# A hybrid decoder block on one core: another order of the projection tiles, and two side jobs as lanes issued by POOL

## The chip, the cores and the metric

The kernel runs on one core of one Trainium2 chip. The metric is the device time of one execution in microseconds. Two executions that were otherwise the same differ by a few microseconds.

## What is computed

A decoder block with two parallel token mixers, all in float32. In the reference, for one layer:

```python
h = _layer_norm(jnp.concatenate([meta, x], axis=1), ln0_g, ln0_b)   # 16 + 1024 rows, 1024 wide
p = h @ w_in[layer] + b_in[layer]                                   # u_s5 | q | k | v | o | i | f | g_s5 | g_m
y_s5 = _s5_mixer(u_s5, ...)                                         # 512 wide, complex diagonal recurrence
z = jax.nn.gelu(y_s5).astype(h.dtype) @ s5_w_glu[layer]
y_s5 = z[..., :D_MODEL] * jax.nn.sigmoid(z[..., D_MODEL:])
hm = _mlstm_mixer(q_h, k_h, v_h, i_pre, f_pre)                      # 4 heads, chunkwise
y_m = (jax.nn.sigmoid(o_pre) * _head_norm(hm)) @ m_w_out[layer]
mix = jax.nn.sigmoid(g_s5) * y_s5 + jax.nn.sigmoid(g_m) * y_m
h = _layer_norm(ALPHA * h + mix @ w_o[layer], ln1_g[layer], ln1_b[layer])
ff = jnp.square(jax.nn.relu(h @ w_up[layer] + b_up[layer])) @ w_down[layer]
h = _layer_norm(ALPHA * h + ff, ln2_g[layer], ln2_b[layer])
```

## The kernel before, in words

**Products.** Every float32 product is made of three passes (`mm3`, L229): each operand is split into a high and a low part, and high × high (L233), high × low (L234) and low × high (L235) are added up in PSUM. The parts of a weight are made on the chip: ACT copies the raw weight into the high part (L219), DVE subtracts it from the raw weight to give the low part (L220). Both go ahead of other work that is ready, so that they stand as early as the scheduler can put them.

**Jobs.** The first half of the kernel is a list of jobs. A job is one tile of 128 columns of a projection, of all 1040 rows, with its weight load on the SP queue, its split, its matmuls and its evacuation. The string `ORDER` (L41) gives their order: `q` and `k` in pairs, `v` (values), `u` (input of the state-space part, S5), `o` (output gate), `g` and `m` (the two mixing gates). Behind them come eight GLU tiles, z0 to z7 (`glu_job`, L927), each of 48 matmuls of 512 columns: their sigmoids are evacuated by ACT (L957, the tile `z2s`), the products with them by DVE (L961, L962). The main loop (L1499) loads the weights two jobs ahead and splits the next job's weight in the middle of each job.

**Lanes.** Everything else in that half, the chunkwise mLSTM heads, the convolution, the S5 tables and recurrence, is written as generators. Each generator hangs in one of seven lanes (`Lane`, L90). After every few matmuls `pump` (L154) moves a clock on by their estimated length and lets every lane whose next step is due run to its next `yield`, whose value says how much later the step after it is due. Those values are the constants at L47 to L62. So the program interleaves side work with the projection matmuls by a table of spacings; the compiler's scheduler may then still move instructions among those that are ready. Two things are forced. An `o` job needs the head that it gates, so the main loop first steps the mLSTM lane until that head is complete (L1512), without matmuls of tiles between. And all lanes are drained before the gate stage (L1537).

**mLSTM chunk steps.** A head goes through its nine chunks with a handful of small matmuls each: transposing k (L465, evacuated by ACT at L467 as `kw`), scores (L470), the output in two parts (L480 from the state `C`, L481), the state's update (L484, into `C` by DVE at L489). One chunk's L480 needs the state that the chunk before it has made. After half a head the rows are normalised (L513) and transposed (L520).

**Two side jobs.** `ah_scale` (L1398) scales the rows of the first layer norm with its gain and bias for a later residual: eight row tiles are loaded, multiplied and added on DVE (L1415), and stored. `up_early` (L1429) prepares three pairs of tiles of the up weights, whose product runs much later with seven products of half-size blocks in place of eight: for each pair it loads two raw tiles (`wur`), makes four combined halves on DVE (`wsums`, L1421 to L1426, the tiles `wus`), and then seven times copies a half on ACT (L1441), subtracts on DVE (L1442, both into `wpre`) and stores the result to DRAM (L1443). Later POOL reads these 21 tiles back (`pre_load`, L1656). Both side jobs hang in one lane, `ah`, one behind the other, and are added at z1. With a spacing of 4 a step, `ah_scale` alone takes 6 + 16 × 4 = 70 of the clock's microseconds.

**The gates.** Behind the GLU tiles `first` splits the first tile of the gate weights (L1064, again a copy on ACT and a subtraction on DVE), and `run7` runs the remaining gate tiles and the output product of the mLSTM, again with seven products of sums of blocks. The sums come from two more lanes: `w_sums` (L975) adds weight blocks by accumulating DMAs on POOL, each behind a 1×1 copy (L989) that waits for a certain job's split; `token_sums` adds row blocks on DVE (L1019, the tiles `rawb`). `early` (at z6) loads the first three weight tiles of the gates.

**Memory.** Nearly all large tiles come from one pool of 30 slots (`slot`, L136): in the GLU stage 18 of them hold the eight mixing tiles, the eight parts of the GELU result and two gates; the weights, their parts and `z2s` hold about seven, and the row blocks of `token_sums` four when it runs. A small ring pool, tag `wr` with four buffers, is opened at z1, when the memory of the mLSTM and S5 lanes is given back.

Of the kernel before, what the change touches and what calls it, by code (L numbers as in the profile page):

```python
# [9 lines left out]
F32 = mybir.dt.float32  # L10
# [4 lines left out]
P = 128  # L15
# [22 lines left out]
LN2_1 = 0.693359375  # L38
LN2_2 = math.log(2.0) - LN2_1
MAGIC = 1.5 * 2 ** 23  # L40
ORDER = "q0 q1 v0 v1 g0 o1 q2 v2 q3 o3 u0 u1 o0 m0 u2 g5 o2 o4 o5 u3 v3 m1 g7 g6 g2 g4 g1 g3 o6 o7"  # L41
S5_START = "v1"
NM = 2
SPLIT_UP = 200
PRE = 3
ZD = 1
ML = [2.87, 1.8, 1.8, 2.49]  # L47
NL = [4, 1.69, 1.5, 2.01]
C5 = [1.7, 2.25, 2.77, 1.57]
K5 = [4.0, 2.0, 2.0, 4.56]  # L50
Z5 = [2.84, 1.51, 1.42, 1.08]
D5 = [6.15, 1.99, 3.44, 2.0]
W5 = [2.01, 3.11, 2.33, 1.5]
Y5 = [3.07, 2.77, 3.44, 1.8]
AFT = 0
AH_START = "z1"
AHY = 4
UPY = 4
PRY = 1.0
TBY = 1.69  # L60
GY = 8.0
GS = 4.0  # L62
VAFT = 2
LOAD0 = "x0 x1 w0 c0 x2 w1 c1 x3 x4 w2 x5 w3 x6"
LN0_PROG = " ".join((
# [54 lines left out]
def decoder_block(  # L120
# [24 lines left out]
    def f32(ap):  # L145
        return ap.bitcast(F32)

    def row_bcast(src, n, off=0):
        return bass.AP(tensor=src.tensor, offset=src.offset + off, ap=[[0, P], [1, n]])
# [1248 lines left out]
    def ah_scale():  # L1398
        gb = [slot("gB0"), slot("bB0")]
        for i in range(2):  # L1400
            nc.sync.dma_start(gb[i][:, :D], row_bcast(ln0r, D, i * D))
        rs = {}
        for t in range(9):
            if t < 8:
                rs[t] = slot("ahr")
                nc.sync.dma_start(rs[t][:, :D], ah0_dr[t * P:(t + 1) * P, :])
            if t == 0:
                yield 4.0
                for i in range(2):
                    v_.tensor_scalar(gb[i][:, :D], gb[i][:, :D], ALPHA, None, op0=OP.mult)  # L1410
                yield 2.0
                continue
            r = rs.pop(t - 1)
            for i, op in enumerate((OP.mult, OP.add)):
                v_.tensor_tensor(r[:, :D], r[:, :D], gb[i][:, :D], op=op)  # L1415
                yield AHY
            nc.sync.dma_start(ah_dr[(t - 1) * P:t * P, :], r[:, :D])

    wu_dr = dram.tile([PRE, 7, P, 1024], F32, name="wu_dr")

    def wsums(a11, a12, a21, a22):  # L1421
        n1, n2 = slot("wus"), slot("wus")
        v_.tensor_tensor(n1[:, 0:512], a21, a22, op=OP.add)
        v_.tensor_tensor(n1[:, 512:1024], n1[:, 0:512], a11, op=OP.subtract)
        v_.tensor_tensor(a21, a11, a21, op=OP.subtract)
        v_.tensor_tensor(n2[:, 0:512], a12, n1[:, 512:1024], op=OP.subtract)  # L1426
        return n1, n2

    def up_early():  # L1429
        for p in range(PRE):  # L1430
            r = [slot("wur"), slot("wur")]
            for j in range(2):
                nc.sync.dma_start(r[j][:, :D], wup[2 * p + j].rearrange("p k f -> p (k f)"))
            yield 3.0
            a11, a12, a21, a22 = r[0][:, 0:512], r[0][:, 512:1024], r[1][:, 0:512], r[1][:, 512:1024]
            n1, n2 = wsums(a11, a12, a21, a22)
            yield 3.0
            for n, w in ((1, a11), (2, a12), (3, n2[:, 0:512]), (4, a22), (5, n1[:, 0:512]), (6, n1[:, 512:1024]),
                         (7, a21)):
                o = slot("wpre", F32R)  # L1440
                a_.activation(o[:, 0:512], w, AF.Copy)  # L1441
                v_.tensor_tensor(o[:, 512:1024], w, f32(o[:, 0:512]), op=OP.subtract)  # L1442
                nc.sync.dma_start(wu_dr[p, n - 1], f32(o[:, 0:1024]))  # L1443
                yield UPY

    for w in ORDER.split():
# [52 lines left out]
    for i, j in enumerate(jobs):  # L1499
# [15 lines left out]
                lanes["ml"].step()  # L1515
        if j.tag == AH_START:
            lanes["ah"].add(ah_scale())
            lanes["ah"].add(up_early())
        if j.tag == "z1":
            mid_ctx.close()  # L1520
            ring_ctx = ExitStack()
            ring[0] = ring_ctx.enter_context(tc.tile_pool(name="ring", bufs=1, side="left"))
        if j.tag == "z2":
            lanes["gp"].add(token_sums())
        if j.tag == "z6":
            early()
        if j.tag == "z7":
            begin()
# [584 lines left out]
```

## Time and profile before

| | us |
|---|---|
| median of three runs (1566.06, 1569.09, 6425.12) | 1569.09 |
| the profiled execution, device time | 1566.52 |
| its span in the trace | 1564.6 |
| PE busy in the span | 1504.2 |
| DVE, ACT, POOL busy | 1065.1, 648.8, 82.0 |
| start of the projections' main part, of z0 to z7, of the gate stage | about 122, 570, 699 |

The trace is of one execution, and its span is 1.9 us shorter than that execution's device time. PE is TensorE's matmuls, PEld its weight loads (which overlap PE), DVE VectorE, ACT ScalarE, POOL GpSimd, and SP the queue of SyncE, which only issues DMAs. A group of instructions is told by line, engine, operation, out<-in and count; behind the bar stand busy time in us and the mean of one in ns, and then the idle time of the engine just before them with what released it. A name as `wpre` stands for all the buffers of that name. The granted clock is TensorE's, 1.00 being full.

### The profile page before, as it was taken

What the parts mean: (1) busy time and instruction counts of PE and PEld (TensorE: products, weight loads), DVE (VectorE), ACT (ScalarE), POOL (GpSimd) and SP (SyncE); (2) the same over time, 40 slices, a digit from 0 to 9 for tenths busy, and PEclk for the clock granted to TensorE, in tenths of its full rate; (3) what the DMA queues carried; (4) which work ended last, traced back from release to release, by engine and by line L of the source; (5) the groups of instructions that cost most, each with busy time, mean ns of one, the idle gap of its engine ahead of it and who ended that gap; (6) DMA issues with size and microseconds to landing.
All of it is one profiled execution on the core that took longest, in us unless ns stands there. A gap on an engine that the chain in (4) does not pass through costs nothing.

```text
span 1564.6 us, 20453 instructions
## 1 busy us (share of the span) xinstructions
PE 1504.2 (96%) x7593; PEld 1272.5 (81%) x7593; DVE 1065.1 (68%) x1957; ACT 648.8 (41%) x991; POOL 82.0 (5%) x183
## 2 busy tenths in 40 slices
PE   8999999999999999919999999999999999999997
PEld 8998899888988877708788888888888888888886
DVE  7785665467673547657789675666666679766786
ACT  6622633354554442135534324444444534433340
POOL 0000000023212000000000001000000000000000
PEclk8999999999999999959999999999999999999999
DMA  8504233323654256587243318644443798667642
GB/s 302 180 24 133 62 78 102 96 81 105 165 111 116 70 167 221 199 347 254 95 148 121 108 63 255 227 154 148 149 150 128 242 370 319 228 225 241 216 169 108
DMA packets 122148, 261.19 MB, mean 167 GB/s; under 512 B 14568, under 2 KB 36784, under 8 KB 122048
## 3 DMA queue, kind: packets, MB, share of 16 engines
q1 hardware_dynamic: 111344, 233.00, 43.6%
q0 software_dynamic: 10704, 26.88, 7.0%
q8 instruction: 60, 0.98, 0.3%
q14 instruction: 40, 0.33, 0.1%
HBM read 188.78 MB, written 84.55 MB: 175 GB/s over the span
## 4 chain that ended last, share of the span: by engine, by line
PE 67%; issue 16%; DMA 2%; ACT 2%; DVE 2%; SPq 0%; POOLq 0%; ACTq 0%; DVEq 0%
PE mm L233 17%; PE mm L235 17%; PE mm L234 17%; PE sd L234 3%; PE sd L235 3%; PE sd L233 3%; DMA wur<-in_wup_dram 1%; PE pn L480 1%; PE pn L481 1%; PE pu L484 1%; DMA wiB<-wrow_dr 1%; PE ln L1600 0%; PE pt L520 0%; ACT gelf L891 0%; PE s5y L874 0%
## 5 line engine op out<-in xcount | busy, mean ns | idle before, releaser
L233 PE MATMUL mm<-hT_hi,whi 128*128 128x512 f32 (+3 forms) x604 | 230.7, 382 | 36.0 <-ACT whi L1064 36.0
L234 PE MATMUL mm<-hT_lo,whi 128*128 128x512 f32 (+3 forms) x604 | 227.8, 377 | 0.0
L235 PE MATMUL mm<-hT_hi,wlo 128*128 128x512 f32 (+3 forms) x604 | 225.3, 376 | 0.1
L233 PEld LDWEIGHTS mm<-hT_hi,whi 128*128 128x128 f32 x604 | 114.2, 189 | 55.2 <-ACT whi L1064 36.8
L235 PEld LDWEIGHTS mm<-hT_hi,wlo 128*128 128x128 f32 x604 | 114.0, 189 | 18.5 <-DVE wlo L1065 0.8
L234 PEld LDWEIGHTS mm<-hT_lo,whi 128*128 128x128 f32 x604 | 114.2, 189 | 16.4
L234 PE MATMUL sd<-dwl,dah 128*128 128x512 f32 x240 | 94.3, 393 | 0.0
L1808 ACT ACTIVATE dah<-da 128x1024 fp32r<-128x1024 f32 x56 | 58.7, 1051 | 85.8 <-PE sd L234 38.2
L233 PE MATMUL sd<-dwh,dah 128*128 128x512 f32 x240 | 94.1, 393 | 0.0
L235 PE MATMUL sd<-dwh,dal 128*128 128x512 f32 x240 | 94.1, 393 | 0.0
L1812 ACT ACTIVATE dwh<-wdr 128x1024 fp32r<-128x1024 f32 x56 | 58.9, 1054 | 83.2 <-DMA wdr<-in_wdn_dram 23.9
L235 PE MATMUL mm<-dwh,dal 128*128 128x512 f32 (+1 forms) x224 | 84.4, 377 | 0.0
L233 PE MATMUL mm<-dwh,dah 128*128 128x512 f32 (+1 forms) x224 | 84.4, 377 | 0.0
L234 PE MATMUL mm<-dwl,dah 128*128 128x512 f32 (+1 forms) x224 | 84.4, 377 | 0.0
L1809 DVE TENSOR_TENSOR dal<-da,dah 128x1024 fp32r<-128x1024 f32 x56 | 68.2, 1220 | 22.9 <-ACT dah L1808 22.9
L1813 DVE TENSOR_TENSOR dwl<-wdr,dwh 128x1024 fp32r<-128x1024 f32 x56 | 68.2, 1220 | 13.6 <-ACT dwh L1812 13.0
L233 PE MATMUL mm<-whi,hT_hi 128*128 128x256 f32 (+1 forms) x256 | 73.5, 287 | 0.0
L234 PE MATMUL mm<-wlo,hT_hi 128*128 128x256 f32 (+1 forms) x256 | 73.3, 286 | 0.0
L235 PE MATMUL mm<-whi,hT_lo 128*128 128x256 f32 (+1 forms) x256 | 73.0, 285 | 0.0
L220 DVE TENSOR_TENSOR wlo<-wraw,whi 128x1024 fp32r<-128x1024 f32 (+1 forms) x46 | 55.9, 1220 | 18.4 <-ACT whi L219 15.6
L219 ACT ACTIVATE whi<-wraw 128x1024 fp32r<-128x1024 f32 (+1 forms) x46 | 48.4, 1057 | 31.6 <-issue 7.1
L235 PE MATMUL mm<-th,wul 128*128 128x512 f32 x156 | 61.4, 394 | 0.0
(478 smaller groups left out, 3672.2 us busy)
## 6 DMA issues: line engine op xcount, KB each, us to landing
da<-act_dr SPq DMA_DIRECT2D x56, 512.0 KB, 6.0
wdr<-in_wdn_dram SPq DMA_DIRECT2D x56, 512.0 KB, 6.2
wur<-in_wup_dram SPq DMA_DIRECT2D x32, 512.0 KB, 4.3
act_dr<-upy SPq DMA_DIRECT2D x64, 256.0 KB, 2.5
wraw<-in_wf_dram SPq DMA_DIRECT2D x30, 512.0 KB, 4.5
wu_dr<-wpre SPq DMA_DIRECT2D x21, 512.0 KB, 5.9
wpre<-wu_dr POOLq DMA_DIRECT2D x21, 512.0 KB, 5.0
act_dr<-upx SPq DMA_DIRECT2D x32, 256.0 KB, 3.6
```

Of the source, the lines that this page charges most:

```text
L219: a_.activation(hi[:, :n], r[:, :n], AF.Copy)
L220: todo.append(lambda e=v_, r=r, hi=hi, lo=lo, n=n: e.tensor_tensor(lo[:, :n], r[:, :n], f32(hi[:, :n]), op=OP.subtract))
L233: t_.matmul(ps, ah, bh, start=(i == 0 and part[0]), stop=False, skip_group_check=skip)
L234: t_.matmul(ps, ah, bl, start=False, stop=False, skip_group_check=skip)
L235: t_.matmul(ps, al, bh, start=False, stop=(i == n - 1 and part[1]), skip_group_check=skip)
L480: t_.matmul(pn[:, :257], qi[:, c0:c0 + n], Cs[c][:, :257], start=True, stop=False)
L481: t_.matmul(pn[:, :257], sws[c], vt[c][:, :257], start=False, stop=True)
L484: t_.matmul(pu[:, :257], kws[c][:n], vt[c][:n, :257], start=True, stop=True)
L1808: a_.activation(ah[:, :D], a[:, :D], AF.Copy)
L1809: v_.tensor_tensor(alo[:, :D], a[:, :D], f32(ah[:, :D]), op=OP.subtract)
L1812: a_.activation(wh, raw[i], AF.Copy)
L1813: v_.tensor_tensor(wl, raw[i], f32(wh), op=OP.subtract)
```

## The change

There are three edits.

1. `ORDER` is another permutation of the same 30 jobs, and the spacings of the lanes are another set of numbers. The `u` tiles, which stood close together (u0 u1, u2, u3), are spread. `S5_START` names another job at the same place of the list.
2. `ah_scale` joins its lane at g6, four jobs ahead of z0, instead of z1, with a spacing of 1.82 for 4. `up_early` stays at z1 with 1.03 for 4, takes its raw and combined tiles from the ring in place of the slots, and the lane is drained ahead of `early` at z6, no longer behind z7. `token_sums` starts at z5 for z2.
3. All 45 DMAs of these two jobs are issued by POOL (`g_`) instead of SP.

```diff
--- before.py
+++ after.py
@@ -38,28 +38,28 @@
 LN2_1 = 0.693359375
 LN2_2 = math.log(2.0) - LN2_1
 MAGIC = 1.5 * 2 ** 23
-ORDER = "q0 q1 v0 v1 g0 o1 q2 v2 q3 o3 u0 u1 o0 m0 u2 g5 o2 o4 o5 u3 v3 m1 g7 g6 g2 g4 g1 g3 o6 o7"
-S5_START = "v1"
+ORDER = "q0 q1 v0 g0 u0 v1 o1 v2 q2 u1 g7 q3 o2 m1 g4 u2 o3 o4 o5 v3 u3 m0 o0 g5 g1 g3 g6 g2 o7 o6"
+S5_START = "g0"
 NM = 2
 SPLIT_UP = 200
 PRE = 3
 ZD = 1
-ML = [2.87, 1.8, 1.8, 2.49]
-NL = [4, 1.69, 1.5, 2.01]
-C5 = [1.7, 2.25, 2.77, 1.57]
-K5 = [4.0, 2.0, 2.0, 4.56]
-Z5 = [2.84, 1.51, 1.42, 1.08]
-D5 = [6.15, 1.99, 3.44, 2.0]
-W5 = [2.01, 3.11, 2.33, 1.5]
-Y5 = [3.07, 2.77, 3.44, 1.8]
+ML = [3.24, 2.49, 1.8, 2.31]
+NL = [1.92, 2.74, 3.59, 2.52]
+C5 = [2.46, 2.46, 1.72, 0.9]
+K5 = [2.43, 5, 2.0, 3.27]
+Z5 = [1.01, 1.84, 1.02, 0.8]
+D5 = [6.04, 2.78, 2.71, 1.81]
+W5 = [4, 1.5, 3.38, 2.29]
+Y5 = [5, 2.96, 2.31, 1.8]
 AFT = 0
-AH_START = "z1"
-AHY = 4
-UPY = 4
-PRY = 1.0
-TBY = 1.69
-GY = 8.0
-GS = 4.0
+AH_START = "g6"
+AHY = 1.82
+UPY = 1.03
+PRY = 1.14
+TBY = 0.93
+GY = 6.81
+GS = 1.5
 VAFT = 2
 LOAD0 = "x0 x1 w0 c0 x2 w1 c1 x3 x4 w2 x5 w3 x6"
 LN0_PROG = " ".join((
@@ -1398,12 +1398,12 @@
     def ah_scale():
         gb = [slot("gB0"), slot("bB0")]
         for i in range(2):
-            nc.sync.dma_start(gb[i][:, :D], row_bcast(ln0r, D, i * D))
+            g_.dma_start(gb[i][:, :D], row_bcast(ln0r, D, i * D))
         rs = {}
         for t in range(9):
             if t < 8:
                 rs[t] = slot("ahr")
-                nc.sync.dma_start(rs[t][:, :D], ah0_dr[t * P:(t + 1) * P, :])
+                g_.dma_start(rs[t][:, :D], ah0_dr[t * P:(t + 1) * P, :])
             if t == 0:
                 yield 4.0
                 for i in range(2):
@@ -1414,12 +1414,15 @@
             for i, op in enumerate((OP.mult, OP.add)):
                 v_.tensor_tensor(r[:, :D], r[:, :D], gb[i][:, :D], op=op)
                 yield AHY
-            nc.sync.dma_start(ah_dr[(t - 1) * P:t * P, :], r[:, :D])
+            g_.dma_start(ah_dr[(t - 1) * P:t * P, :], r[:, :D])
 
     wu_dr = dram.tile([PRE, 7, P, 1024], F32, name="wu_dr")
 
-    def wsums(a11, a12, a21, a22):
-        n1, n2 = slot("wus"), slot("wus")
+    def wsums(a11, a12, a21, a22, early=False):
+        if early:
+            n1, n2 = (ring[0].tile([P, 1024], F32, tag="wr", bufs=4, name="wus") for _ in range(2))
+        else:
+            n1, n2 = slot("wus"), slot("wus")
         v_.tensor_tensor(n1[:, 0:512], a21, a22, op=OP.add)
         v_.tensor_tensor(n1[:, 512:1024], n1[:, 0:512], a11, op=OP.subtract)
         v_.tensor_tensor(a21, a11, a21, op=OP.subtract)
@@ -1428,19 +1431,19 @@
 
     def up_early():
         for p in range(PRE):
-            r = [slot("wur"), slot("wur")]
+            r = [ring[0].tile([P, 1024], F32, tag="wr", bufs=4, name="wur") for _ in range(2)]
             for j in range(2):
-                nc.sync.dma_start(r[j][:, :D], wup[2 * p + j].rearrange("p k f -> p (k f)"))
+                g_.dma_start(r[j][:, :D], wup[2 * p + j].rearrange("p k f -> p (k f)"))
             yield 3.0
             a11, a12, a21, a22 = r[0][:, 0:512], r[0][:, 512:1024], r[1][:, 0:512], r[1][:, 512:1024]
-            n1, n2 = wsums(a11, a12, a21, a22)
+            n1, n2 = wsums(a11, a12, a21, a22, True)
             yield 3.0
             for n, w in ((1, a11), (2, a12), (3, n2[:, 0:512]), (4, a22), (5, n1[:, 0:512]), (6, n1[:, 512:1024]),
                          (7, a21)):
                 o = slot("wpre", F32R)
                 a_.activation(o[:, 0:512], w, AF.Copy)
                 v_.tensor_tensor(o[:, 512:1024], w, f32(o[:, 0:512]), op=OP.subtract)
-                nc.sync.dma_start(wu_dr[p, n - 1], f32(o[:, 0:1024]))
+                g_.dma_start(wu_dr[p, n - 1], f32(o[:, 0:1024]))
                 yield UPY
 
     for w in ORDER.split():
@@ -1515,14 +1518,15 @@
                 lanes["ml"].step()
         if j.tag == AH_START:
             lanes["ah"].add(ah_scale())
-            lanes["ah"].add(up_early())
         if j.tag == "z1":
             mid_ctx.close()
             ring_ctx = ExitStack()
             ring[0] = ring_ctx.enter_context(tc.tile_pool(name="ring", bufs=1, side="left"))
-        if j.tag == "z2":
+            lanes["ah"].add(up_early())
+        if j.tag == "z5":
             lanes["gp"].add(token_sums())
         if j.tag == "z6":
+            lanes["ah"].drain()
             early()
         if j.tag == "z7":
             begin()
```

Lines behind L1415 of the old kernel stand three or four lines lower in the new one: the copies of `up_early` at L1441 are now at L1444, the loads at L1436, the stores at L1446, the read-backs at L1660.

**Place 1: ACT at the end of the GLU tiles.** L957 is a sigmoid evacuation of a GLU tile, L219 the next tile's weight copy, L1064 the first gate split. Before:

```order
L957 ACTIVATE z2s<-mm 128x512
L219 ACTIVATE whi<-wraw 128x1024
L957 ACTIVATE z2s<-mm 128x512 x3
L1441 ACTIVATE wpre<-wur 128x512 x2
L1441 ACTIVATE wpre<-wus 128x512
L1441 ACTIVATE wpre<-wur 128x512
L1441 ACTIVATE wpre<-wus 128x512 x2
L1441 ACTIVATE wpre<-wur 128x512 x3
...
L1441 ACTIVATE wpre<-wus 128x512 x2
L1441 ACTIVATE wpre<-wur 128x512
L1064 ACTIVATE whi<-wraw 128x1024
```

Now (L1014 is a copy of `token_sums`):

```order
L957 ACTIVATE z2s<-mm 128x512 x2
L219 ACTIVATE whi<-wraw 128x1024
L1444 ACTIVATE wpre<-wur 128x512
L957 ACTIVATE z2s<-mm 128x512
...
L1444 ACTIVATE wpre<-wus 128x512 x2
L1014 ACTIVATE hT_hi<-rawb 128x2x512
L1444 ACTIVATE wpre<-wur 128x512
L1014 ACTIVATE hT_hi<-rawb 128x2x512
L957 ACTIVATE z2s<-mm 128x512 x2
L219 ACTIVATE whi<-wraw 128x1024
L957 ACTIVATE z2s<-mm 128x512
L1064 ACTIVATE whi<-wraw 128x1024
L957 ACTIVATE z2s<-mm 128x512
```

The 21 copies stood in one piece between the last GLU evacuation and the first gate split. Now they stand among the evacuations of z2 to z6, and the gate split stands ahead of z7's last sigmoid. z7's own split (the last L219) has two copies of `token_sums`, a preparation copy and z6's sigmoids right ahead of it.

**Place 2: PE where o1 forces mLSTM head 0.** The numbers are those of tiles: `pn` and `pu` are outputs and updates of one chunk. Before, three chunk steps in a row with no other matmul between (the first and the last of them, without the middle one's rows):

```order
L465 MATMUL pk_1801<-ident_74,kT_1051 128x128
L470 MATMUL pS_1805<-qT_969,kT_1051 128x128
L480 MATMUL pn_1809<-C_1791,qi_1668 128x257
L481 MATMUL pn_1809<-v12_882,sw_1784 128x257
L484 MATMUL pu_1812<-v12_882,kw_1780 128x257
...
L480 MATMUL pn_1855<-C_1837,qi_1668 128x257
L481 MATMUL pn_1855<-v12_883,sw_1830 128x257
L484 MATMUL pu_1858<-v12_883,kw_1826 128x257
L520 MATMUL pt_1884<-ident_74,hraw_1768 128x128
```

Now two:

```order
L465 MATMUL pk_1960<-ident_74,kT_1045 128x128
L470 MATMUL pS_1964<-qT_967,kT_1045 128x128
L480 MATMUL pn_1968<-C_1950,qi_1617 128x257
L481 MATMUL pn_1968<-v12_880,sw_1943 128x257
L484 MATMUL pu_1971<-v12_880,kw_1939 128x257
L465 MATMUL pk_1983<-ident_74,kT_1045 128x128
L470 MATMUL pS_1987<-qT_967,kT_1045 128x128
L480 MATMUL pn_1991<-C_1973,qi_1617 128x257
L481 MATMUL pn_1991<-v12_881,sw_1966 128x257
L484 MATMUL pu_1994<-v12_881,kw_1962 128x257
L520 MATMUL pt_2020<-ident_74,hraw_1904 128x128
```

The step that is gone from here now stands between matmuls of earlier tiles.

**Place 3: POOL from the end of the projections on.** `ws_dr` are the weight sums, each behind its `mark`. Before:

```order
L989 COPY mark<-whi 1x1
L991 DMA ws_dr<-ws_dr 128x4x512
L989 COPY mark<-whi 1x1
L991 DMA ws_dr<-in_wmo_dram 128x4x512
L1656 DMA wpre<-wu_dr 128x1024 x21
```

Now:

```order
L989 COPY mark<-whi 1x1
L991 DMA ws_dr<-ws_dr 128x4x512
L1417 DMA ah_dr<-ahr 128x1024
L1436 DMA wur<-in_wup_dram 128x1024 x2
L1406 DMA ahr<-ah_dr 128x1024 x2
...
L989 COPY mark<-whi 1x1
L991 DMA ws_dr<-in_wmo_dram 128x4x512
L1446 DMA wu_dr<-wpre 128x1024 x2
...
L1446 DMA wu_dr<-wpre 128x1024 x11
L1660 DMA wpre<-wu_dr 128x1024 x21
```

The rows of both side jobs have gone from SP's order to POOL's; the last pair of a mark and a sum stands between the loads and the first stores of `up_early`.

## The prediction

> **What bounds the kernel now.** I read the profile's first part before anything else. PE is busy for 1504 of 1565 us, so a change of order or of queues can only win where PE waits or runs at a low clock.
>
> ```profile
> span 1564.6 us, 20453 instructions
> PE 1504.2 (96%) x7593; PEld 1272.5 (81%) x7593; DVE 1065.1 (68%) x1957; ACT 648.8 (41%) x991; POOL 82.0 (5%) x183
> ```
>
> Next comes the list of PE's waits, by line and releaser. One entry outweighs all others together: a single wait of 36.0 us for the first weight split of the gate stage (L1064).
>
> ```profile
> PE mm L233 <- ACT whi L1064: 36.0, 1, 36.0
> PE pS L470 <- ACT kw L467: 2.5, 4, 1.0
> PE pt L520 <- DVE hraw L513: 2.3, 1, 2.3
> PE mm L233 <- ACT whi L219: 1.9, 2, 1.0
> PE pn L480 <- DVE C L489: 1.0, 1, 1.0
> ```
>
> The third view is busy time by stage. Its columns: window and length, then busy us (and instructions) of PE, PEld, DVE, ACT, POOL, then PE's granted clock, DMA share and GB/s. The stages are the head, the projection tiles, the GLU tiles z0 to z7, the hole, and everything from the gate stage to the end.
>
> ```profile
> 122.00:570.00 448.00, 441.58 (x2525) 389.86 (x2524) 271.01 (x665) 199.97 (x317) 60.14 (x118) 1.00 0.39 104
> 570.00:663.00 93.00, 90.94 (x395) 72.66 (x393) 58.81 (x65) 20.17 (x28) 1.45 (x2) 1.00 0.62 209
> 663.00:699.00 36.00, 0.14 (x1) 0.00 (x0) 23.00 (x38) 12.44 (x22) 0.00 (x0) 0.53 0.87 330
> 699.00:1565.00 866.00, 856.90 (x3772) 697.82 (x3772) 618.03 (x900) 356.69 (x534) 12.33 (x22) 0.99 0.55 188
> ```
>
> In the hole PE does 0.14 us of work, while DVE and ACT do 23 and 12 us and the DMA engines are 87% busy. The chain of waits says with what: three rounds of loading a pair of up weights, combining and splitting it (`up_early`, L1429), and then the one split that PE waits for.
>
> ```profile
> 662.93 4.69 DMA wur<-in_wup_dram
> 671.27 5.04 DMA wur<-in_wup_dram
> 685.20 7.48 DMA wur<-in_wup_dram
> 695.96 2.17 ACT wpre L1441 x4
> 698.13 0.96 ACT whi L1064
> 699.13 0.79 PE mm L233
> 699.92 0.43 PE mm L234
> 702.48 0.41 PE mm L235
> 702.89 0.23 PE mm L233
> ```
>
> The hole is thus no lack of data for the gates. All 21 preparation copies stand ahead of the first gate split in ACT's order, and they trickle in at the pace of the loads. The last rows show a second, small cost: eight matmuls start between 699.13 and 702.71 at 0.43 us apart rather than 0.23, under the lowered clock (0.53 in the hole's window). That is 3.58 us for 8 × 0.23 = 1.83, so 1.75 us.
>
> **The change, part by part.** From the first gate split on, the order of the instructions on PE, DVE, ACT and SP is the same as before, and so it is on PE up to the place where v1's first matmuls stood:
>
> ```profile
> 100.39 1.09 PE L347 MATMUL mm<-whi,meta_hl 128*48 128x256 f32 x8
> ```
>
> So the 865.5 us from 699.1 on and some 100 us at the front stay, as long as nothing late flows in. The sum is about what lies between.
>
> *The hole.* In the new order of ACT all 21 copies stand between z2's and z7's evacuations, and the first gate split stands right behind, in the middle of z7. What the hole contained is not removed; it goes under z1 to z6. Here is what must hide there:
>
> ```profile
> L1442 DVE TENSOR_TENSOR wpre<-wur,wpre 128x512 fp32r<-128x512 f32 x12 | 8.0, 684 | 0.0
> L1441 ACT ACTIVATE wpre<-wur 128x512 fp32r<-128x512 f32 x12 | 7.1, 617 | 13.2 <-DMA wur<-in_wup_dram 12.8 <-DVE wpre L1442 0.3
> L1442 DVE TENSOR_TENSOR wpre<-wus,wpre 128x512 fp32r<-128x512 f32 x9 | 5.9, 684 | 0.0
> L1441 ACT ACTIVATE wpre<-wus 128x512 fp32r<-128x512 f32 x9 | 5.3, 619 | 14.2 <-DVE wus L1426 14.2
> L1423 DVE TENSOR_TENSOR wus<-wur 128x512 f32<-128x512 f32 x3 | 2.1, 692 | 12.9 <-DMA wur<-in_wup_dram 12.9
> L1415 DVE TENSOR_TENSOR ahr<-ahr,gB 128x1024 f32<-128x1024 f32 x8 | 9.8, 1222 | 5.8 <-DMA ahr<-ah_dr 5.7
> L1415 DVE TENSOR_TENSOR ahr<-ahr,bB 128x1024 f32<-128x1024 f32 x7 | 8.6, 1222 | 0.1
> ```
>
> DVE: 8.0 + 5.9 + 4 × 2.1 (L1423 to L1426) = 22.3 us come in. The scaled rows (L1415, 9.8 + 8.6 us, last two rows, in z1 to z7 before) leave for the projections from g6 on. The stage z0 to z7 then has 58.8 − 18.4 + 22.3 = 62.7 us of DVE in 93, and ACT 20.2 + 12.4 = 32.6. The projections have 271 + 18 = 289 of 448. Neither is full.
>
> Transfers: 6 loads and 21 stores of 0.5 MB are 14.2 MB. Over the roughly 66 us of z1 to z6 (six tiles of 48 matmuls at 0.23 = 11.0 us) that is 215 GB/s. The 8.4 MB of scaled rows (8 loads, 8 stores, 127 GB/s over the same time) leave. From the stage's 209 GB/s that makes about 297, and the hole itself ran at 330. It fits, without much to spare. So the hole goes whole: **−36.0**. With it goes the low clock behind it: **−1.75**. If part of the cover fails, each microsecond by which the last copy misses z7 comes back one for one.
>
> *From SP to POOL.* 45 DMAs change queue. POOL's own price for one is in the rows below: 0.54 us for a 512-KB load, so 45 × 0.54 = 24 us of an engine that has 1.45 us to do in z0 to z7. SP loses the same work. Behind these DMAs on POOL stand only the last two copies of the sum lane (L989 and L991), whose results the gates need 12 us and more later, and the 21 read-backs of L1656, which come hundreds of microseconds later. By itself I cost this at 0, between 0 and the price in the second rival.
>
> ```profile
> L1656 POOL DMA_DIRECT2D wpre<-wu_dr x21 | 11.2, 538 | 387.1 <-DMA woraw<-in_wo_dram 239.8 <-PE mm L235 140.6 <-PE sd L235 6.8
> 582.03 0.17 POOL L989 COPY mark<-whi 1x1 f32<-1x1 f32 x1 [33.91 <-ACT whi L219]
> 386.01 2.83 POOL L989 COPY mark<-whi 1x1 f32<-1x1 f32 x1 [1.49 <-ACT whi L219]
> wu_dr<-wpre SPq DMA_DIRECT2D x21, 512.0 KB, 5.9
> ```
>
> The Trainium skill speaks against the queue as a cause: "DMA: Bandwidth & Descriptors", section "Issuing engines are not separate DMA queues", says that all DMAs run on the same 16 engines and interleave, whoever starts them, and that spreading the issuers saves only sequencer time. By that rule the queue edit alone leaves the time where it is, and the order alone brings the gain; the trace agrees as far as it goes, since the hole's DMA share is 0.87 on SP's queue.
>
> *The projection tiles.* The matmuls are the same ones, so only waits can be won or lost. 448 − 441.6 = 6.4 us of idling stand in the second window, most of it where o1 forces the rest of mLSTM head 0 without tiles between: three chunk steps in a row.
>
> ```profile
> 155.39 0.27 PE L465 MATMUL pk<-ident,kT 128*128 128x128 f32 x1
> 156.18 0.49 PE L470 MATMUL pS<-qT,kT 128*128 128x128 f32 x2 [0.52 <-ACT kw L467]
> 157.80 0.27 PE L465 MATMUL pk<-ident,kT 128*128 128x128 f32 x1
> ```
>
> One step is 157.80 − 155.39 = 2.41 us, of which about 1.6 is work: 0.8 idle. In the new order two such steps stand at o1, not three: **−0.8**. The transposes behind them (the 2.3-us wait for L513) stand as they stood. I cannot price each of the other places where S5 and mLSTM pieces have moved. From below, all 6.4 us could go, and with them some 1.7 us of low clock around o1 (160 to 168 us, estimated from 0.8 more steps' worth); from above, the idling could double. I take −0.8, with −8 to +6 as the bounds: the row of this place is the only one that I can count.
>
> *The GLU tiles.* Before, two tiles start late, by 1.0 us each, on their weight split (1.9 in the list of waits). Now z7's split stands behind z6's evacuations and behind a preparation copy that needs a slot freed late in z5. I estimate one late start of about 1.4 us in place of two of 1.0: **−0.5**. For 49 added small instructions between the evacuations of z2 to z7 I add **+1.0**, bounds 0 (DVE stands at 62.7 of 93) and +15 (if all of ACT's 12.4 us, and more, stood in front of late splits).
>
> Sum, against the profiled execution: 1566.5 − 36.0 − 1.75 − 0.8 − 0.5 + 1.0 = **1528.5 us**. That execution (1566.52) lies 2.6 us under the median of the three runs (1569.09) and 0.5 over the lowest (1566.06); I put the new median at the new profiled time.
>
> **The rivals.** *Half a hole (12%).* The last round still ends after z7. For it: in the chain it takes 698.13 − 685.20 = 12.9 us from the load to the last copy, and the z stage has the DMA engines 62% busy already. Against it: ACT's order puts the last copies in z5 and z6, a tile ahead of z7's split. Price: 12.9 us come back, 1541.4.
>
> *POOL held by DVE (5%).* The 1×1 copy takes 0.17 us when DVE is quiet and 2.83 at 386 us. If each issue on POOL were held as long, 27 DMAs take 27 × (0.54 + 2.66) = 86 us, against 66 us of z1 to z6: 20 us come back, 1548.5. Against it: the 64 issues of L783 amid full projections took 0.52 us each on average. The Trainium skill, "GPSIMD Engine Reference", section "1. Specifications", has POOL share its SBUF interfaces with VectorE, in contention when a VectorE instruction has two SBUF inputs; almost all of the 49 added ones on DVE have, and the two copy rows agree with it, but no row here shows an issue held.
>
> ```profile
> L783 POOL DMA_DIRECT2D s5Mx<-s5Kt x64 | 32.6, 521 | 27.7 <-ACT s5RS L774 12.7 <-ACT whi L219 9.3 <-DMA ws_dr<-in_wf_dram 2.4
> ```
>
> *The other side: stores in series (3%).* Each prepared weight holds one of the 30 slots through its copy, its subtraction and its store: 0.6 + 0.7 + 5.9 = 7.2 us by the rows above. 18 slots hold the mix, GELU and gate tiles, some 7 the weights and gates of the z tiles. If one slot is left, 21 × 7.2 = 151 us must fit in 66, and 85 come back: 1613, slower than before. With two it is 76, and 10 come back. It makes the change a loss above (66 + 38) / 21 = 5.0 us per weight. Against it: the four further slots that `early` takes for the gates' rows are claimed only after this lane is drained, so some five are free until then.
>
> *Less waiting than I count (15%).* If no GLU tile starts late and half of the projections' idling and low clock goes, it is 1528.5 − 2.4 − 2.8 − 0.9 = 1522.4; with no wait at all, 1528.5 − 2.4 − 5.6 − 1.7 = 1518.8.
>
> *The new order costs (7%).* S5 pieces come late for z0 or a projection; the idling doubles: 1528.5 + 6 = 1534.5.
>
> **How the numbers follow.** The forecast itself has 58%. The low end, 1520, leaves out only the end of "less waiting"; the high end, 1543, takes in half a hole. What is left out (the held POOL, the series, and a part of each neighbour) is some 2 in 10. Two per cent, about what a measurement of this kernel can tell from no change, is 31.4 us: faster means under 1537.7. The forecast, "less waiting" and "the new order costs" lie below it (58 + 15 + 7 = 80%). Half a hole and the held POOL are within 2% (17%). Slower means over 1600.5, which only the series reaches (3%).
>
> **What would show it.** Right: the list of PE's waits has no entry for L1064 above 2 us, the clock stays at 1.00 across the gates' start, and the gate stage begins near 662 us; between its start and the end lie about 864 us. DVE stays near 63 us in z0 to z7, and POOL's DMA rows near 0.54 us. A first gate matmul later than 675 us, or POOL rows of 2 us and more, make me wrong in the way that the rivals name; waits by S5 or mLSTM lines between 100 and 570 us of over 10 us together make the projections the step that failed.

## The result and the profile after

The changed kernel takes **1539.6 us** (median of four runs, 1538.3 to 1541.5); the kernel before, run beside it, takes 1568.5. The ratio is 0.982 (95% interval 0.980 to 0.984). (One of the four runs before took 6425.1 us and is not in the ratio.) That is 29 us gained where 40 were forecast: inside the range, 11 us above the point. A median under 1537.7 us, two per cent faster, to which the prediction gave 80%, was not reached. The profiled execution took 1540.39 us, its span is 1538.6.

Busy time by stage in the kernel after, columns as before (window and length; PE, PEld, DVE, ACT, POOL; clock, DMA share, GB/s). z0 now starts at 583, the gate stage at 673.6.

```profile
122.00:583.00 461.00, 446.60 (x2599) 394.55 (x2598) 287.75 (x696) 192.55 (x315) 64.99 (x134) 0.99 0.41 114
583.00:673.60 90.60, 89.33 (x386) 71.96 (x385) 68.08 (x87) 31.66 (x49) 18.26 (x33) 1.00 0.89 308
673.60:1538.60 865.00, 855.66 (x3773) 696.52 (x3771) 618.08 (x900) 356.86 (x533) 12.31 (x22) 1.00 0.54 184
```

The hole has no row any more. The GLU stage is a little shorter than before, the tail as long. The surprise is the first row: the projections have 461.0 − 446.6 = 14.4 us of idling where 6.4 stood, and z0 starts 12.8 us later than before (first recorded matmuls 583.14 and 570.31). PE's waits in the kernel after say where:

```profile
PE pt L520 <- DVE hraw L513: 5.8, 2, 3.4
PE ln L1290 <- ACT x L1278: 4.8, 2, 3.6
PE mm L235 <- DVE wlo L220: 4.6, 3, 2.3
PE pS L470 <- ACT kw L467: 2.0, 3, 1.0
PE ln L1352 <- DVE ident L162: 1.6, 1, 1.6
PE s5z L819 <- DVE s5Z L827: 1.6, 1, 1.6
```

The wait of 36.0 us for L1064 is gone from the list. New are three waits for the low part of a weight (L220, 4.6 us in all), a second wait for the transposes (L520) and one for S5. Ahead of z0, the waits on mLSTM and S5 lines add up to 10.6 us (6.3 before), those for L220 to 3.6 (none before): these are the 8 us of added idling. For the other 4.8 of the 12.8 us PE is busy longer. Eight transposes that stood in z0 before (1.0 us) and more time at a low clock are part of that; the rest is not resolved.

And the first gate matmuls run at full clock, 0.23 us apart (PE in the kernel after):

```profile
673.63 0.40 PE L233 MATMUL mm<-hT_hi,whi 128*128 128x512 f32 x1
673.87 0.40 PE L234 MATMUL mm<-hT_lo,whi 128*128 128x512 f32 x1
674.10 0.39 PE L233 MATMUL mm<-hT_hi,whi 128*128 128x512 f32 x1
```

The difference between the two executions, followed along the kernel: z0 is 12.8 us late; the hole brings 36.0 and the GLU stage 2.3, so the gate stage starts 25.5 us early (673.63 for 699.13); eight matmuls later the lead is 27.25; at the end it is 26.0.

**Where the late weights come from.** Four rows of DVE and one of PE in the kernel after, in order of time:

```profile
543.26 0.48 DVE L489 SCALAR_TENSOR_TENSOR C<-C,dec,pu 128x257 f32<-128x257 f32 x1 [0.41 <-PE pu L484]
551.01 0.69 DVE L1410 TENSOR_SCALAR bB<-bB 128x1024 f32<-128x1024 f32 x1 [7.00 <-DMA bB<-in_ln0r_dram]
556.73 1.21 DVE L1415 TENSOR_TENSOR ahr<-ahr,bB 128x1024 f32<-128x1024 f32 x1
558.00 1.23 DVE L220 TENSOR_TENSOR wlo<-wraw,whi 128x1024 fp32r<-128x1024 f32 x1
559.28 0.50 PE L235 MATMUL mm<-hT_hi,wlo 128*128 128x512 f32 x1 [2.30 <-DVE wlo L220]
```

DVE stands still for 7.0 us, because the next instruction in its order scales the bias row, whose load has not landed. Then it works off the scaled rows, and the weight part that PE needs (558.00) comes behind them. In the list of DMAs this load takes 11.2 us from issue to landing, where the gain row, issued 2.1 us earlier, took 3.6. Between the two, POOL issued an accumulating weight sum of 1 MB. Below are the row of the list, POOL's order, and the stages in which the load was on its way: the DMA engines were busy all the time (share 1.00 and 1.06).

```profile
bB<-in_ln0r_dram POOLq DMA_DIRECT2D x1, 512.0 KB, 11.2
```

```profile
538.17 1.33 POOL L991 DMA_DIRECT2D ws_dr<-in_wmo_dram  x1
539.75 0.57 POOL L1401 DMA_DIRECT2D bB<-in_ln0r_dram  x1 [0.25 <-DVE wlo L220]
```

```profile
540.00:545.00 5.00, 5.00 (x25) 4.20 (x24) 2.48 (x8) 2.62 (x4) 1.40 (x3) 1.00 1.00 180
545.00:550.00 5.00, 5.00 (x24) 4.15 (x23) 0.00 (x0) 0.15 (x1) 0.00 (x0) 1.00 1.06 325
```

Issuing as such costs POOL 0.54 us a piece, as before (groups of POOL in the kernel after):

```profile
L1446 POOL DMA_DIRECT2D wu_dr<-wpre x21 | 11.2, 537 | 50.5 <-DVE wpre L1445 50.1
```

**Where the transposes wait.** At 405 us, o4 forces the end of mLSTM head 2. The 3.4 us of idling are followed by some 4 us of low clock. Stages of 4 us in the kernel after:

```profile
400.00:404.00 4.00, 1.53 (x7) 0.94 (x5) 1.43 (x7) 2.05 (x3) 0.00 (x0) 1.00 0.00 0
404.00:408.00 4.00, 3.04 (x15) 3.04 (x16) 1.83 (x8) 1.63 (x3) 0.00 (x0) 0.65 0.02 4
408.00:412.00 4.00, 4.00 (x33) 3.63 (x32) 2.90 (x3) 3.97 (x6) 1.90 (x2) 0.92 0.34 35
```

The kernel before had one such place in the projections (o1, 160 to 168 us); the one after has o1 and this.

### The profile page after: what moved, and what is told of

Its sections match the earlier page's. It is cut to its first block, busy times and chain, and to the rows that moved or that the text cites. A ratio compares the mean times of both kernels' runs of the same rounds, so it can differ in the third digit from the quotient of the medians.

```text
span 1538.6 us, 20470 instructions
## 1 busy us (share of the span) xinstructions
PE 1505.4 (98%) x7593; PEld 1272.1 (83%) x7593; DVE 1065.2 (69%) x1957; ACT 644.5 (42%) x990; POOL 104.4 (7%) x228
## 4 chain that ended last, share of the span: by engine, by line
PE 58%; issue 28%; DVE 5%; DMA 4%; ACT 2%; POOL 1%; SPq 0%; POOLq 0%; DVEq 0%; ACTq 0%
PE mm L235 14%; PE mm L234 14%; PE mm L233 14%; PE sd L234 3%; PE sd L233 3%; PE sd L235 3%; DMA x<-in_x_dram 1%; DMA wpre<-wu_dr 1%; DMA ah_dr<-ahr 1%; PE pn L480 1%; PE mm L1334 1%; PE pn L481 1%; PE pu L484 1%; DMA wiB<-wrow_dr 1%; PE s5y L875 0%
## 5 line engine op out<-in xcount | busy, mean ns | idle before, releaser
L1813 DVE TENSOR_TENSOR dal<-da,dah 128x1024 fp32r<-128x1024 f32 x56 | 68.1, 1220 | 23.0 <-ACT dah L1812 22.4
L1817 DVE TENSOR_TENSOR dwl<-wdr,dwh 128x1024 fp32r<-128x1024 f32 x56 | 68.2, 1220 | 12.9 <-ACT dwh L1816 12.2
L220 DVE TENSOR_TENSOR wlo<-wraw,whi 128x1024 fp32r<-128x1024 f32 (+1 forms) x46 | 56.1, 1222 | 25.4 <-ACT whi L219 22.6
L234 PE MATMUL mm<-tl,wuh 128*128 128x512 f32 x156 | 61.4, 394 | 0.0
```

What stands on the lines that cost most here:

```text
L220: todo.append(lambda e=v_, r=r, hi=hi, lo=lo, n=n: e.tensor_tensor(lo[:, :n], r[:, :n], f32(hi[:, :n]), op=OP.subtract))
L234: t_.matmul(ps, ah, bl, start=False, stop=False, skip_group_check=skip)
L1813: v_.tensor_tensor(alo[:, :D], a[:, :D], f32(ah[:, :D]), op=OP.subtract)
L1817: v_.tensor_tensor(wl, raw[i], f32(wh), op=OP.subtract)
```

## The experiments

Theory A at the outset: the 12.8 us are two separate losses in the projections, the forced end of head 2 (an effect of the order) and late weights behind the scaled rows (an effect of the side jobs). Rivals: all of it is the order, or all of it the side jobs. Every run in one table; start of z0 and of the gate stage, the length of the GLU stage and of what follows (span − gate start) are from the profiles, in us. In the rows before and e1 the GLU stage contains the hole. The positions come from one execution of each kernel, and whole times of one kernel differ by 2 to 7 us; a difference of one or two us between two rows says nothing.

| run | z0 | GLU stage | gates | rest | median | ratio to before (95%) |
|---|---|---|---|---|---|---|
| before | 570.3 | 128.8 | 699.1 | 865.5 | 1568.5 | 1 |
| after | 583.1 | 90.5 | 673.6 | 865.0 | 1539.6 | 0.982 (0.980 to 0.984) |
| e1_order_only | 577.8 | 128.0 | 705.7 | 866.0 | 1574.5 | 1.004 (1.002 to 1.005) |
| e2_lanes_only | 578.5 | 92.9 | 671.4 | 864.7 | 1538.8 | 0.981 (0.980 to 0.982) |
| e3_sp_queue | 581.3 | 88.8 | 670.2 | 866.0 | 1536.6 | 0.980 (0.978 to 0.981) |
| e4_first_use_late | 579.6 | 107.2 | 686.8 | 864.9 | 1552.1 | 0.989 (0.988 to 0.991) |
| e5_u3_ahead | 582.1 | 91.3 | 673.4 | 863.5 | 1539.9 | 0.981 (0.980 to 0.983) |
| e6_early_loads | 584.0 | 90.8 | 674.7 | 865.1 | 1541.7 | 0.982 (0.981 to 0.984) |
| e7_early_loads_u3 | 580.5 | 94.6 | 675.2 | 863.9 | 1541.0 | 0.982 (0.981 to 0.984) |
| e8_early_loads_u3_sp | 580.0 | 90.3 | 670.2 | 864.0 | 1538.6 | 0.980 (0.979 to 0.982) |
| e9_old_order_rows_late | 571.9 | 89.9 | 661.8 | 879.0 | 1542.2 | 0.983 (0.982 to 0.985) |
| e10_rows_late | 576.5 | 89.1 | 665.6 | 878.5 | 1547.0 | 0.987 (0.985 to 0.990) |
| e11_old_order_sp | 583.7 | 90.1 | 673.8 | 864.7 | 1540.0 | 0.982 (0.980 to 0.983) |
| e12_both_under_z | 570.2 | 108.1 | 678.2 | 865.9 | 1547.4 | 0.987 (0.985 to 0.989) |

### The two halves of the change

**e1_order_only**: the old kernel with the new order and the new spacings.

```diff
-ORDER = "q0 q1 v0 v1 g0 o1 q2 v2 q3 o3 u0 u1 o0 m0 u2 g5 o2 o4 o5 u3 v3 m1 g7 g6 g2 g4 g1 g3 o6 o7"
+ORDER = "q0 q1 v0 g0 u0 v1 o1 v2 q2 u1 g7 q3 o2 m1 g4 u2 o3 o4 o5 v3 u3 m0 o0 g5 g1 g3 g6 g2 o7 o6"
...
-ML = [2.87, 1.8, 1.8, 2.49]
+ML = [3.24, 2.49, 1.8, 2.31]
```

> The kernel before with the new order of the projection tiles and the new spacings of the mLSTM and S5 lanes alone; both side jobs stay as they were. Theory A (two separate losses in the projections: a forced end of mLSTM head 2 ahead of o4, about 5.5 us of waiting and low clock, and late weight splits behind the scaled rows, about 4.7 us): only the first belongs to this edit, with 1.6 us at an S5 product and 1.0 of transposes that now stand ahead of z0. z0 starts at about 578.5 us (570.1 before, 583.1 after), the 36-us wait at L1064 stays, and the time is 1566.5 + 8 = about 1575. Theory B (the order alone costs the whole 12.6 us): z0 at 583, time 1579. Theory C (the side jobs cost all of it): z0 at 570, time 1567.

z0 starts at 577.8, near A's 578.5. The whole is 5.2 us slower than before, less than the 8 expected, and clear of zero. The new order by itself is a loss.

**e2_lanes_only**: the changed kernel with the old order and spacings.

```diff
-ORDER = "q0 q1 v0 g0 u0 v1 o1 v2 q2 u1 g7 q3 o2 m1 g4 u2 o3 o4 o5 v3 u3 m0 o0 g5 g1 g3 g6 g2 o7 o6"
+ORDER = "q0 q1 v0 v1 g0 o1 q2 v2 q3 o3 u0 u1 o0 m0 u2 g5 o2 o4 o5 u3 v3 m1 g7 g6 g2 g4 g1 g3 o6 o7"
...
-AH_START = "g6"
+AH_START = "g1"
```

> The changed kernel with the old order of the projection tiles and the old spacings of the mLSTM and S5 lanes; the side jobs as changed, the scaled rows starting at the fourth tile ahead of z0 (here g1). Theory A: the hole goes (no wait at L1064), no wait for transposes near 400 us, but late weight splits of up to 4.7 us ahead of z0 and in it: z0 at about 574, time about 1531. Theory B: z0 at 570, time about 1528. Theory C: z0 at 582 or later, time about 1539.

The hole is gone without the new order, and the time is that of the full change (intervals overlap). So the side jobs bring the whole gain; which part of their edit removes the hole (the rows out of the lane, the shorter spacing, the ring, the earlier drain) was not taken apart. But z0 stands at 578.5, not 574: they cost the projections 8.2 us here, and theory A was too low. The halves do not add: 7.5 and 8.2 us of delay alone, 12.8 together.

### The queue, and the time of the loads

**e3_sp_queue**: all 45 DMAs of the side jobs back on SP.

```diff
-                g_.dma_start(rs[t][:, :D], ah0_dr[t * P:(t + 1) * P, :])
+                nc.sync.dma_start(rs[t][:, :D], ah0_dr[t * P:(t + 1) * P, :])
```

> The changed kernel with the 45 DMAs of the side jobs issued by SP again. Theory A, with the queue as the reason (the bias rows took 11.2 us to land because they stand behind an accumulating DMA of 1 MB on POOL's queue, and DVE stood 7.0 us at its first use): the bias lands in about 5 us, the late weight splits at 556, 571 and 584 us go, time 1540.4 - 4.7 = about 1536. Rival (all queues share the same engines, so the queue changes nothing): 1540 and the same waits. Rival (SP's own stream of weights falls behind the side jobs' stores, which wait for DVE): z tiles wait for their weights, over 1545.

1536.6 us, as theory A had it; its interval and that of the change just overlap. The waits for L220 fall from 4.6 to 0.7 us, z0 comes 1.8 us earlier. In the list of DMAs the bias row lands sooner, and DVE's wait for it (second row, DVE's waits from 535 to 600 us) falls from 7.0 to 3.1:

```profile
bB<-in_ln0r_dram SPq DMA_DIRECT2D x1, 512.0 KB, 8.1
```

```profile
DVE bB L1410 <- DMA bB<-in_ln0r_dram: 3.1, 1, 3.1
```

**e11_old_order_sp** puts the same question to the old order (e2 with the same edit).

> Old order and spacings of the projections, side jobs as changed (the scaled rows in the last projections), all 45 DMAs issued by SP. If SP's gain of 3 us in the new order was that the bias rows land sooner, the same happens here, where DVE waits 4.0 us for them and their transfers took 10.4 and 10.9 us: 1538.8 - 3 = about 1536, z0 at about 575.5. Rival (the queue does nothing by itself): 1539, z0 at 578.5.

It does not repeat. The two rows take 5.5 and 8.3 us to land, yet DVE's waits for them add up to 4.9 us (4.0 in e2); z0 is 5.2 us later than in e2, the GLU stage 2.8 shorter, the time the same. In the old order a bias row that lands sooner thus brings nothing. The trade of POOL for SP thus has no sign that holds in both orders. The Trainium skill, "DMA: Bandwidth & Descriptors", section "Issuing engines are not separate DMA queues", would have the queue change next to nothing; e11 against e2 agrees, e3 against the change differs by 3.0 us.

**e4_first_use_late**: 12 us more of the lane's clock between the loads and DVE's first use.

```diff
-                yield 4.0
+                yield 16.0
```

> The changed kernel with the scaled rows' first step on DVE set 16 instead of 4 lane microseconds behind its loads. Theory A: DVE no longer waits at its head for the bias rows (7.0 us now), the late weight splits at 556, 571 and 584 us go, time about 1536. Rival (the splits are late because DVE is full there, whatever it waits for): the L220 waits stay at 4.6 us and more, time 1540.

The waits for L220 ahead of z0 are gone, and z0 comes 3.5 us earlier, about what they had cost (3.6). But theory A's condition was not met: the scaling of the bias row moved only from 551.0 to 551.9 us, and DVE still waits 5.3 us for it and 1.8 for the gain row. What changed is that the weight part now stands ahead of that wait in DVE's order (545.4), and that six of the rows' steps, not ten, stand ahead of z0. And the run is 12.5 us slower than the change. PE's waits in e4:

```profile
PE mm L233 <- ACT whi L219: 11.8, 1, 11.8
```

That is z7's weight split: the whole side lane runs later, and its last copies stand ahead of the split in ACT's order. This is the prediction's rival "half a hole" (priced there at 12.9 us), and it shows how little room the lane has: 12 us more on the lane's clock cost a wait of 11.8.

**e6_early_loads**: the lane starts one tile earlier, the loads too; the arithmetic was meant to stay about where it was.

```diff
-AH_START = "g6"
+AH_START = "g3"
...
-                yield 4.0
+                yield 16.0
```

> The changed kernel with the side lane started one tile earlier (g3), and the scaled rows' first DVE step 16 instead of 4 lane microseconds behind their loads: the loads are some 11 us earlier, the DVE steps about where they were, POOL still issues. Theory A (DVE stands at its head until the bias rows have landed, and the weight splits are late behind that): DVE's wait for gB and bB below 1.5 us (7.0 now), L220 waits below 1 us (4.6 now), z7 in time, unlike in the run with the later first use: about 1536. Rival (DVE is full there): 1540 with the same L220 waits. Rival (z7 late again): 1548 or more.

The bias row is loaded 14 us earlier, but DVE's first steps also move forward (its scaling from 551.0 to 532.3 us), and its waits for the two rows are 4.3 us, not below 1.5. The late weights shrink to 0.8, but nothing is won (1541.7). First DVE's largest wait of 540 to 575 us in e6, then new entries among PE's waits:

```profile
DVE ahr L1415 <- DMA ahr<-ah_dr: 11.8, 2, 7.1
```

```profile
PE pn L480 <- DVE C L489: 2.3, 1, 2.3
PE mm L233 <- ACT whi L219: 1.9, 1, 1.9
```

DVE now waits at its head for a row instead of the bias, up to 7.1 us; behind it stands the state `C` of a chunk step instead of a weight, and PE waits 2.3 us for that. The wait has changed its name.

### The forced end of head 2

**e5_u3_ahead** gives head 2 one more tile of cover.

```diff
-ORDER = "q0 q1 v0 g0 u0 v1 o1 v2 q2 u1 g7 q3 o2 m1 g4 u2 o3 o4 o5 v3 u3 m0 o0 g5 g1 g3 g6 g2 o7 o6"
+ORDER = "q0 q1 v0 g0 u0 v1 o1 v2 q2 u1 g7 q3 o2 m1 g4 u2 o3 u3 o4 o5 v3 m0 o0 g5 g1 g3 g6 g2 o7 o6"
```

> The changed kernel with one tile moved in the order: u3 stands ahead of o4 instead of behind v3, so that mLSTM head 2 has a tile more before o4 forces its end. Theory A (the forced end costs 3.4 us of waiting for the transposes, 0.6 behind it and 1.5 of low clock): the L520 wait near 401 us and the clock below 1.00 at 404 to 412 us go, time 1540.4 - 5 = about 1535.5. Rival (the wait only moves, to another chunk step or another head's end): 1539 to 1541, with a new wait of 3 us on an mLSTM line.

The wait only moves. PE's waits in e5:

```profile
PE pt L520 <- DVE hraw L513: 4.2, 2, 2.3
PE s5y L875 <- DVE s5w L863: 2.4, 1, 2.4
PE mm L233 <- DVE v L361: 2.2, 1, 2.2
```

The wait for head 2's transposes falls from 3.4 to 1.8 us, and two new ones of 2.4 and 2.2 us stand at an S5 product and at a value tile, each on DVE. The time is unchanged. Theory A's price for this place was right as a reading of one wait, and wrong as a gain to be had by moving a tile.

**e7_early_loads_u3** joins e5 and e6, **e8_early_loads_u3_sp** adds SP's queue (edits as above).

> Both edits of the two runs before together, POOL still issues. Theory A (two separate losses): they add, 1540.4 - 5 - 4 = about 1531. Rival (the two places share one cause, so one repair does for both): 1535 to 1536, no better than each alone.

> The same with the 45 DMAs issued by SP. If the queue matters only through the late bias rows, nothing is left for it once the loads are early: 1531, as the run before. Rival (the 3.8 us that SP's queue brought come from something else as well): about 1527. Rival (SP's weights fall behind stores that wait for DVE): over 1535.

Nothing adds up: 1541.0 and 1538.6. Theory A, as two repairable places, falls. SP's queue is worth 2.4 us here, near the 3.0 of e3 and against the old order. The next question was not where the scaled rows wait, but what they cost as a whole.

### The scaled rows elsewhere

Theory A2: the loss by the side jobs ahead of z0 is that of the scaled rows, wherever in the projections they stand. **e9_old_order_rows_late** (on e2) and **e10_rows_late** (on the changed kernel) put them behind the first gate split.

```diff
-AHY = 1.82
+AHY = 4
...
-        if j.tag == AH_START:
-            lanes["ah"].add(ah_scale())
...
     for l in lanes.values():
         l.drain()
+    lanes["ah"].add(ah_scale())
     first()
     run7()
+    lanes["ah"].drain()
```

> Old order and spacings of the projections; the up weights prepared under the GLU tiles as in the changed kernel; the scaled rows taken out of the projections and put behind the first gate split, as a lane with 4 us a step through the gate stage (they are read only when the gates are done). Theory A2 (the side jobs' loss ahead of z0 comes from the scaled rows alone, whose DVE steps wait at the head of DVE for their loads while chunk steps and weight splits stand behind): z0 at 570 to 571 (578.5 with the rows in the projections), no hole, 1538.8 - 8 = about 1530.5. Rival (the loss comes from elsewhere, say the earlier preparation or memory slots): z0 stays at 577 or later, 1537 to 1540. Rival (the gate stage pays what the projections save, since its evacuations stand behind the same waits): z0 at 570, but the gate stage longer by 4 us and more, 1535 and over.

> The changed kernel with its new order, and the scaled rows moved behind the first gate split in the same way. Theory A2: z0 at 577.8, where the run with the new order alone had it (583.1 in the changed kernel), no wait for L220 ahead of z0, 1539.6 - 5.4 = about 1534. Rival (the loss comes from elsewhere): z0 at 582 to 583, 1539.

Stages of e2, then of e9:

```profile
122.00:578.50 456.50, 444.65 (x2535) 390.74 (x2533) 282.50 (x677) 196.58 (x315) 68.67 (x132) 1.00 0.41 116
578.50:671.40 92.90, 90.07 (x385) 71.89 (x386) 69.96 (x91) 34.08 (x52) 18.10 (x34) 1.00 0.90 312
671.40:1536.00 864.60, 855.73 (x3773) 696.72 (x3771) 617.75 (x900) 356.76 (x533) 12.30 (x22) 1.00 0.54 184
```

```profile
122.00:571.90 449.90, 442.92 (x2543) 391.11 (x2543) 271.85 (x669) 200.17 (x317) 60.29 (x118) 1.00 0.39 104
571.90:661.80 89.90, 89.77 (x394) 72.88 (x393) 62.11 (x84) 31.93 (x50) 17.53 (x32) 1.00 0.84 297
661.80:1540.80 879.00, 861.10 (x3773) 698.38 (x3771) 637.39 (x918) 357.08 (x533) 20.31 (x37) 0.99 0.55 191
```

A2 holds in both orders, for z0: it moves from 578.5 to 571.9 in the old, from 583.1 to 576.5 in the new. That it is 6.6 us each time is chance, by the spread above. How the rows cost it differs: in the new order 3.6 us of waits for L220 go with them, in the old the waits that go stand on ACT (L470, L219, L465). With the rows away, the GLU stage carries the up weights and PE is busy for 89.8 of 89.9 us; the gates start at 661.8, where the prediction had them. But the last row has grown from 864.6 to 879.0: the gate stage now pays 14.4 us, the rival's case. In e10 it is the same (878.5 for 865.0): 1547.0, where 1534 was expected. PE's waits in e9:

```profile
PE mm L235 <- DVE wlo L1065: 5.8, 3, 3.8
PE mm L233 <- ACT whi L1064: 3.1, 4, 1.1
```

There, too, the weight splits stand among the rows and the steps of `token_sums`. But here DVE does not stand still: it is busy for all of the 4 us from 708 to 712, so what stands ahead of the splits is work, not a wait for a load. The clock falls behind these waits (0.73 and 0.84 between 712 and 720 us).

**e12_both_under_z** lets both side jobs share the GLU stage, on e2, with the rows in a lane of their own.

```diff
-AH_START = "g1"
-AHY = 1.82
+AH_START = "z1"
+AHY = 4
...
-            lanes["ah"].add(ah_scale())
+            lanes["cv"].add(ah_scale())
```

> Old order and spacings of the projections; the scaled rows at z1 with 4 us a step, where the kernel before had them, but in a lane beside the preparation of the up weights, so that both side jobs share z1 to z7. Theory A3 (the scaled rows cost nothing in the GLU stage only because the stage has room for one side job; the bytes of both are 19.4 MB + 14.2 MB = 33.6 MB, at the hole's 330 GB/s 102 us against a stage of 90): z0 at 570 to 571, no hole, late weights or late preparation in z5 to z7, the stage about 102 us long, time about 1538 (1533 to 1545). Rival (both fit, DVE at 81 of 93 us, DMA at 365 GB/s): z0 at 570 to 571, stage of 90 us, time about 1528.5, the forecast itself.

The GLU stage of e12, then PE's waits in the same run:

```profile
570.20:678.20 108.00, 93.95 (x393) 74.69 (x392) 76.81 (x97) 33.28 (x50) 24.98 (x46) 0.95 0.86 310
```

```profile
PE mm L233 <- ACT whi L219: 11.1, 3, 6.8
PE mm L235 <- DVE wlo L220: 3.0, 2, 2.6
```

z0 is back at 570.2, so the projections are as before, and the stage is 108 us long, even more than theory A3 made it (102); the time, 1547.4, lies above A3's range too. It has room for one of the two jobs. Whether bytes alone make it so is not settled: the DMA engines were 86% busy, and ACT's copies waited for stores to give slots back as well (ACT's waits in e12 from 570 to 679 us):

```profile
ACT wpre L1444 <- DMA wu_dr<-wpre: 14.2, 5, 6.7
```

## Why the prediction was right, and where not

- **The hole, −36.0: right.** No wait for L1064 is left; e2 shows that the side jobs alone remove it, and in e4, with the lane delayed, the preparation is late again and PE waits 11.8 us for it.
- **The low clock behind it, −1.75: right**: the lead grows from 25.5 to 27.25 us over the eight first matmuls.
- **What must hide in the GLU stage: right in kind.** DVE was put at 62.7 us and has 68.1, since seven of the rows' sixteen steps still run there; in e9, where none does, it has 62.1. 297 GB/s were forecast, 308 measured; but that sum adds a rate over 93 us and two over 66. By bytes it is 19.4 + 14.2 − 8.4 = 25.2 MB in 90.5 us, 278 GB/s, and that 297 came near is luck. The stage took 90.5 us for 92.8 (without the hole) before: −2.3, where −0.5 and +1.0 had been put down. PE's waits for weights went from 1.9 to 1.3 us there, as the −0.5 had it; the +1.0 for added instructions did not show (the prediction counts 49 of them on DVE; its own rows give 33, and 21 on ACT). 1.0 more of the gain is only moved: eight transposes that now stand ahead of z0.
- **POOL: right.** 0.54 us an issue; POOL held by DVE did not happen. What stands *ahead* on the queue was not asked: the bias row was issued behind an accumulating DMA.
- **The chunk step at o1: right in kind.** Two waits of 0.52 us are left there, of three; what went is a wait of 0.5, not 0.8.
- **The projection tiles, −0.8 with bounds of −8 to +6: this step failed.** Only the one place was counted, and for the scaled rows nothing was put down, by the sentence "The projections have 271 + 18 = 289 of 448. Neither is full." z0 starts 12.8 us late, beyond the upper bound. In the new order 6.6 us of this go when the scaled rows go (after against e10), 4.6 when the order goes too (e10 against e9), and 1.6 are left to the rest of the edit (e9 against before); taken in other steps the shares differ, as the halves do not add (e1: the order alone 7.5). DVE, put at 64% busy, was taken for an engine with room. At the place shown above it stood 7.0 us with nothing to do before a load, its later instructions behind it, and PE then waited 2.3 us for one of them. How much of the 6.6 us comes from such standing, and how much from the rows' own 12 us of work on DVE, no run separates: with the waits for L220 ahead of z0 down to 0.7 and 0, z0 comes 1.8 and 3.5 us earlier (e3, e4), and in the old order e11 shows no gain.
- **The signs named ahead.** No wait for L1064, a full clock at the gates' start and 865 us behind it came as said. The gate stage began at 673.6, not near 662, and the waits on S5 and mLSTM lines between 100 and 570 us add up to 10.6: the prediction's own sign, over 10 us, that the projections are the step that failed.
- **The tail, 0: nearly.** Of the lead of 27.25 us, 26.0 are left at the end; 0.7 goes where the up product reads the prepared weights back, 0.4 of it in a new wait for the first of them; the rest is spread.

The sum as measured: −36.0 − 1.75 + 12.8 − 2.3 + 1.25 = −26.0. That the point is missed by no more than 12 us owes something to the GLU stage, which came out better than put down. "The new order costs" was among the rivals, at +6, which is about what the order costs (4.6 to 7.5); that the scaled rows cost something in the projections was not. Where the kernel before had them, PE waited 1.9 us in all in the GLU stage, and the change gave that place to the up weights: it buys 37.75 us for 6.6 of the rows and some 5 to 7 of the order. The order brings nothing that a run here shows: e2 without it is as fast.

## What to carry to other kernels

A side job is priced by the stage into which it goes, and a job that makes room for it must be priced again where it lands: the same 16 steps came with at most 1.9 us of PE's waits in the GLU stage of the kernel before, cost 6.6 us in the projections and 14 in the gate stage. A share of busy time says little about room on an engine that works off its instructions in order, as DVE does at 544 to 558 us above; ask for each added instruction whether its data are there when it comes to the head, and what PE needs behind it. And a wait that ends last is not a gain until a run shows that the next one does not take its place: three repairs here (e5, e6, e7) moved waits and not the time, a fourth (e4) cost 12.5 us, and only e3 may have brought some.

## What the hardware showed beyond that

The same two 512-KB broadcast loads stand at different places in these runs. Issued by POOL within 2 us behind an accumulating sum of 1 MB, each took 10.2 to 12.1 us to land (six loads: one in the kernel after, two in e2, one in e4, two in e12). All others took 3.6 to 8.3 us: on POOL with no accumulating sum right ahead (such as 3.6 for the gain row in the kernel after, 6.4 and 6.8 in e9, 8.2 behind a plain copy of 1 MB in e7), and on SP even while a sum was under way (4.3 and 8.1 in e3, 5.5 and 8.3 in e11). So the place behind the sum in POOL's order delays a load, even if the whole kernel's time shows no constant sign of it.

A wait of PE of 2 to 3 us is often followed by 4 to 8 us at a granted clock of 0.6 to 0.9 (404 to 412 us in the kernel after), but not after each: behind the 2.3 us at 559 the clock stayed at 1.00. Even the same wait differs: behind the 2.3 us for the transposes at o1 it fell to 0.64 (164 to 168 us) in the kernel before and to 0.57 (176 to 180 us) in the one after, and stayed at 1.00 in e1 and e2. What decides between the two is open.
